# The opening of a decoder block: the exponential behind the root, one quarter of the squares on VectorE, the root ahead of the weight's split, the first value products by high parts first

## The chip, the cores and the metric

The kernel runs on one core of a Trainium2 chip. That core has TensorE (matrix products, PE in the profile), VectorE (DVE), ScalarE (ACT), GpSimd (POOL), SyncE (SP, which issues most loads) and 16 DMA engines. The metric is the device time of one execution in microseconds; less is better. A time before or after is the median of several executions.

## The reference

One layer of a hybrid decoder block on 2048 tokens of width 1024, all in float32. A conditioning vector gives a shift, a scale and a gate; the normed input is projected to eight pieces; one branch is a gated linear recurrence (RG-LRU), the other attention over three dilated windows; both are merged and added to the input.

```python
mod = c_act @ w_mod[l] + b_mod[l]                       # c_act = silu(c)
shift, scale, gate = jnp.split(mod, 3, axis=-1)
h = rms_norm(x, g_norm[l]) * (1.0 + scale[:, None, :]) + shift[:, None, :]
proj = h @ w_in[l]
x_rnn, z_rnn, q, k, v, z_attn, g_r, g_a = jnp.split(proj, IN_SPLITS, axis=-1)
...                                                     # conv, RG-LRU, attention, merge
x = x + gate[:, None, :] * (merged @ w_o[l])
return rms_norm(x, g_final)
```

`rms_norm` divides each row by the root of its mean square. In the RG-LRU, `log_a = -8 * r * softplus(-lam)`; `softplus(-lam)` is a constant of 1024 channels.

## The kernel before

Each large product is done in three matmuls: a number is split in a high part that TensorE takes exactly and a low part, and high by high, high by low and low by high are summed (`mm3`). For a weight, ScalarE copies the high part (`hi_act`, L162) and GpSimd subtracts it from the whole for the low part (`lo_pool`, L168); for the activations VectorE subtracts (`lo_dve`, L171). `S` are the tiles of split weights.

All products use a Strassen-like scheme on blocks of the sequence and the width. The order of the work isn't left to a scheduler: it is the order in which the program is written, engine by engine. An engine works through its own list, and waits at an instruction until what that needs is there. SyncE issues the loads in the written order.

The opening, lines 614 to 865, brings the first 512 rows of x (`x0`, four row sets of 128 rows by 1024) to a normed and shifted form, and makes the first products, of the values v, with them. Its parts are:

- `decay_constants` (L681) makes the constant `softplus(-lam)` on 128 x 8 elements. It is a generator, and is continued by `next(decay)`. ScalarE makes the exponential (L690), VectorE a series in 25 small operations (L694 to L705). Before each function of another family ScalarE loads a table (`ACT_TABLE_LOAD`).
- The squares of x0 (L711 to L713) are summed by row on ScalarE. `rstd_first` (L173) forms the mean on VectorE and the square root on ScalarE (L176). `rstd_last` (L178) inverts it and refines it with one Newton step on 128 x 4 elements (L180 to L184). `scale_rows` (L782) multiplies the rows of x, the first 256 columns of all four row sets first, the other 768 later.
- `mod_rows`, `mod_products` and `mod_turned` compute `c_act @ w_mod`, 256 columns of shift and scale at a time (index j from 0 to 3). Of eight blocks of 128 rows of the weight, ScalarE and VectorE sum the first 3, 4, 6 or 8 (by j) scaled by `ca` into `acc` (L730, L734), TensorE takes the others. The sum leaves as a row, `mrow` (ScalarE, L745), is turned to a column by eight one-column matmuls, and VectorE adds the bias (`mod`, L755) and the gain (`gs`, L756).
- `even(j)` transposes two blocks of 128 columns of x0 on TensorE (`turned`, L542). For each, ScalarE applies scale and shift twice, once to the high part (L552) and once to the full number (L556), and VectorE subtracts for the low part (L171).
- `value_sums(j, units)` (L766) adds to six sums in PSUM, called X, X, Z, W, V, Y, the products of those two blocks, 12 matmuls of 128 x 256 for each sum; the two X come first.
- `splits(m, j)` splits a weight tile of v, and loads the next. `idle_matmuls(n)` runs n matmuls of no use on a constant tile.

The PSUM pool `pg` has two buffers. Every tile that is asked from it, of `idle_matmuls`, `mod_products`, `mod_turned` and `turned` alike, waits until the tile before the last has been read.

Of the kernel before, what the change touches and what calls it, by code (L numbers as in the profile page):

```python
# [15 lines left out]
ALU = mybir.AluOpType  # L16
# [73 lines left out]
def decoder_block(ctx, tc, x, c, positions, g_norm, w_mod, b_mod, w_in, b_gate, conv_w, conv_b,  # L90
# [62 lines left out]
    def mm(o, l, r, st, sp, **kw):  # L153
        nc.tensor.matmul(o, lhsT=l, rhs=r, start=st, stop=sp, **kw)  # L154
# [18 lines left out]
    def rstd_first(ss):  # L173

        nc.vector.tensor_scalar(ss[:, 0], ss[:, 0], 1.0 / D, EPS, ALU.mult, ALU.add)
        nc.scalar.activation(ss[:, 1], ss[:, 0], AF.Sqrt)  # L176
# [451 lines left out]
    def load_mod(j):  # L628
        for q in range(2):
            w_m[q, j] = t = T(hp, [P, KT, 256], F32, "T", bufs=14)  # L630
            c0 = q * D + j * 256
            nc.sync.dma_start(t[:], w_mod[0, :, c0 : c0 + 256].rearrange("(k p) m -> p k m", p=P))
# [35 lines left out]
    def splits(m, j):  # L668
        split_raw(m, j)
        if ahead:  # L670
            load_raw(*ahead.pop(0))
# [11 lines left out]
    def decay_constants():  # L683
        nc.vector.tensor_scalar(hb[:], par[:, C_BG : C_BG + 16], 0.5, None, ALU.mult)
        la = par[:, C_LAM : C_LAM + 8]
        e1 = T(cp, [P, 8], F32, "e1")
        e2 = T(cp, [P, 8], F32, "e2")
        e3 = T(cp, [P, 8], F32, "e3")
        nc.vector.scalar_tensor_tensor(e1[:], la, -1.0, la, ALU.mult, ALU.min)
        nc.scalar.activation(e1[:], e1[:], AF.Exp)  # L690
        yield
        nc.vector.tensor_scalar(e2[:], e1[:], 2.0, None, ALU.add)
        nc.vector.reciprocal(e2[:], e2[:])
        nc.vector.tensor_tensor(e1[:], e1[:], e2[:], ALU.mult)  # L694
        nc.vector.tensor_tensor(e2[:], e1[:], e1[:], ALU.mult)
        nc.vector.tensor_scalar(e3[:], e2[:], 1.0 / 19, 1.0 / 17, ALU.mult, ALU.add)
        for d in (15, 13, 11, 9, 7, 5, 3, 1):
            if d == 9:
                yield
            nc.vector.tensor_tensor(e3[:], e3[:], e2[:], ALU.mult)  # L700
            nc.vector.tensor_scalar(e3[:], e3[:], 1.0 / d, None, ALU.add)
        nc.vector.tensor_tensor(e3[:], e3[:], e1[:], ALU.mult)
        nc.vector.tensor_scalar(e1[:], la, -1.0, 0.0, ALU.mult, ALU.max)
        nc.vector.scalar_tensor_tensor(e1[:], e3[:], 2.0, e1[:], ALU.mult, ALU.add)
        nc.vector.tensor_scalar(sp8[:], e1[:], 8.0, None, ALU.mult)  # L705
# [2 lines left out]
    next(decay)  # L708
    ssx = T(vx, [P, 3, 4], F32, "ssx", bufs=2)
    nc.scalar.activation(ssx[:, 1, 0:1], ones[:], AF.Sqrt)  # L710
    for r in range(4):  # L711
        jk = T(vx, [P, D], BF16, "hf", bufs=2)
        nc.scalar.activation(jk[:], x0[r], AF.Square, accum_out=ssx[:, 0, r : r + 1])  # L713
    load_mod(2)
    splits(0, 0)
    load_mod(3)

    mod = T(cp, [P, 2, KT], F32, "mod")
    sh = mod[:, 0, :]
# [39 lines left out]
    def even(j):  # L759
        for k in (2 * j, 2 * j + 1):  # L760
            build(vx, ("B11", "B21"), x0, k, True, pt=turned(x0, k))
# [4 lines left out]
    def value_sums(j, units):  # L766

        for m, g in units:
            for r in range(2):
                js = slice((2 * g + r) * P, (2 * g + r + 1) * P)  # L770
                for k in (2 * j, 2 * j + 1):
                    (hh, hl), w = B[("B11", "B21")[k // KH]], w_v[m, j]
                    mm3(sums[m, g][:, r, :], hh[:, k % KH, js], hl[:, k % KH, js], w[:, 0, k % 2], w[:, 1, k % 2],
                        first=j == 0 and r == 0 and k == 0, last=j == 3 and k == KT - 1, skip_group_check=True)

    def squares(xs):
        ss = T(vx, [P, 3, 4], F32, "ssx", bufs=2)
        for r in range(4):
            jk = T(vx, [P, D], BF16, "hf", bufs=2)
            nc.scalar.activation(jk[:], xs[r], AF.Square, accum_out=ss[:, 0, r : r + 1])  # L780
        return ss

    def scale_rows(xs, ss, rows=range(4), cols=slice(0, D)):
        for r in rows:
            nc.vector.tensor_scalar(xs[r][:, cols], xs[r][:, cols], ss[:, 1, r : r + 1], None, ALU.mult)
# [10 lines left out]
    def first_values():  # L796

        odd = build_odd(vx, x1)
        units = list(sums)
        for q in range(2):  # L800
            mod_rows(0, q)
        next(decay)
        mod_products(0)
        idle_matmuls(3)
        rstd_first(ssx)
        splits(1, 0)
        x1.extend(load_x(hp, 1, "T", 14))
        rstd_last(ssx)
        scale_rows(x0, ssx, cols=slice(0, 2 * P))
        mod_turned(0)  # L810
        even(0)
        for q in range(2):
            mod_rows(1, q)
        splits(2, 0)
        scale_rows(x0, ssx, cols=slice(2 * P, D))
        mod_rows(2, 0)
        next(decay, None)
        for j in range(4):
            for i, (m, g) in enumerate(units):
                value_sums(j, [(m, g)])  # L820
                if j < 3 and g:
                    splits(m, j + 1)
                if j == 3:
                    if i:
                        store_values(vx, *old, sums[old[0], old[2]])
                    old = m, 0, g
                    if i < 4:
                        split_raw(3, i)
                    if i in (3, 5):
                        next(odd)  # L830
                if (j, i) == (2, 1):
                    ss = squares(x1)
                    rstd_first(ss)
                if i == 2 and j < 3:
                    mod_products(j + 1)
                    if j == 2:
                        rstd_last(ss)
                        scale_rows(x1, ss, range(2))
                if i == 3 and j < 3:
                    mod_turned(j + 1)  # L840
                    even(j + 1)
                    if j == 0:
                        mod_rows(2, 1)
                        mod_rows(3, 0)
                        mod_rows(3, 1, 0, 4)
                    elif j == 1:
                        mod_rows(3, 1, 4)
                    else:
                        scale_rows(x1, ss, range(2, 4))
        spare[0] = True  # L850
        plan = {(t, i): [] for t in range(5) for i in range(4)}
        for i in range(4):
            plan[0, i].append(lambda i=i: load_piece(0, i))
            for t in range(1, 4):
                plan[t, i].append(lambda t=t, i=i: split_piece(t - 1, i))
                if t < 3:
                    plan[t, i].append(lambda t=t, i=i: load_piece(t, i))
            plan[4, i].append(lambda i=i: products(i - 4))
        for t, i in ((0, 0), (0, 2), (1, 0), (1, 1), (1, 3), (2, 0), (2, 1), (2, 3), (3, 0), (3, 1)):
            plan[t, i].append(lambda: next(odd))  # L860
        plan[3, 2].append(lambda: (next(odd, None), products(-8)))
        plan[3, 3].append(lambda: products(-5))
        evicts = [lambda: store_values(vx, *old, sums[old[0], old[2]])]
        value_runs(vx, ((3, 0), (3, 1), (0, 1), (1, 1), (2, 1)), plan, evicts)
        products(0)
# [1478 lines left out]
```

## Time and profile before

| | us |
|---|---|
| median of 3 executions | 2202.35 (2197.92, 2202.59, 2202.35) |
| the profiled execution | 2203.34 |
| its span, first to last instruction | 2200.7 |
| TensorE busy in the span | 2161.4 (98%) |
| VectorE, ScalarE, GpSimd busy | 1488.3, 1261.9, 1237.5 |
| first high part of x0 starts (ScalarE, L552) | 23.57 |
| second mod read (VectorE, L755) | 40.31 |

In the rows of a timeline the first number is the start in microseconds from the start of the span and the second the duration of all instructions of the row (xN at its end is their count). Then come the engine, the line, the operation, and what it writes and reads. A bracket gives the idle time of the engine just before, and what ended it.

### The profile page before, as it was taken

How to read it: one execution, taken by the hardware profiler on the slowest of the kernel's cores; microseconds unless marked ns; L12 is line 12 of the kernel's file. 1: busy time of each engine (PE TensorE's matmuls, PEld its weight loads, DVE VectorE, ACT ScalarE, POOL GpSimd, SP SyncE). 2: the span in 40 equal slices, each digit the busy share in tenths (PEclk: the TensorE clock that was granted, in tenths of full speed). 3: DMA queues.
4: the chain of work that ended last, by engine and by line, in shares of the span. 5: the costliest groups of instructions: out<-in, count | busy, mean ns of one | idle time of the engine just before them, and what ended most of it. 6: DMA issues, size and time to landing. Idle time of an engine off the chain costs nothing. (4 is left out here: it accounts for less than half of the span.)

```text
span 2200.7 us, 34270 instructions
## 1 busy us (share of the span) xinstructions
PE 2161.4 (98%) x11330; PEld 1838.1 (84%) x11330; DVE 1488.3 (68%) x2453; ACT 1261.9 (57%) x2543; POOL 1237.5 (56%) x910
## 2 busy tenths in 40 slices
PE   8999999999999999999999999999999999999998
PEld 5998888888888998888888887888889898978786
DVE  6678888978576765455545465467677878755876
ACT  4647667667543447557557412567778887632433
POOL 2468767677566355445445223446575656433886
PEclk9999999999999999999999999999999999999999
DMA  8355665665897567787887898989988888799453
GB/s 291 103 172 185 219 198 194 203 209 195 265 274 221 166 191 255 248 250 233 263 258 248 263 286 274 284 267 273 289 272 270 242 257 255 226 291 296 160 164 134
DMA packets 454522, 513.89 MB, mean 234 GB/s; under 512 B 91241, under 2 KB 333637, under 8 KB 453577
## 3 DMA queue, kind: packets, MB, share of 16 engines
q1 hardware_dynamic: 427444, 431.81, 65.2%
q10 hardware_dynamic: 26708, 79.86, 9.4%
q8 instruction: 89, 1.46, 0.3%
q14 instruction: 89, 0.72, 0.1%
q0 software_dynamic: 192, 0.05, 0.0%
HBM read 337.52 MB, written 174.07 MB: 232 GB/s over the span
## 5 line engine op out<-in xcount | busy, mean ns | idle before, releaser
L168 POOL TENSOR_TENSOR S<-R,S 128x512 fp32r<-128x512 f32 x278 | 411.4, 1485 | 372.2 <-ACT S L162 271.2
L154 PE MATMUL V<-T,S 128*128 128x512 f32 x1344 | 324.4, 390 | 0.5 <-DVE xr L482 0.5
L154 PE MATMUL X<-T,S 128*128 128x512 f32 x1344 | 323.3, 389 | 0.3 <-POOL S L168 0.3
L154 PEld LDWEIGHTS X<-T,S 128*128 128x128 f32 x1344 | 252.0, 188 | 52.9 <-POOL S L168 0.7
L154 PEld LDWEIGHTS V<-T,S 128*128 128x128 f32 x1344 | 251.4, 188 | 52.9 <-DVE xr L482 1.0
L154 PE MATMUL pj<-yh,S 128*128 128x512 f32 x848 | 287.6, 397 | 4.4 <-ACT yh L162 3.8
L168 POOL TENSOR_TENSOR S<-s,S 128x512 fp32r<-128x512 f32 x114 | 183.0, 1605 | 103.2 <-ACT S L162 78.7
L162 ACT ACTIVATE S<-R 128x512 fp32r<-128x512 f32 x278 | 171.2, 622 | 117.1 <-DMA R<-in_w_in_dram 77.4
L154 PEld LDWEIGHTS pj<-yh,S 128*128 128x128 f32 x848 | 160.7, 190 | 37.5 <-ACT yh L162 4.7
L1596 ACT ACTIVATE pp<-pp,st 128x256 f32<-128x256 f32 (+3 forms) x256 | 133.4, 523 | 75.4 <-DVE st L1595 75.0
L154 PE MATMUL pj<-yl,S 128*128 128x512 f32 x424 | 167.5, 395 | 2.4 <-DVE yl L171 1.5
L154 PE MATMUL Y<-T,S 128*128 128x512 f32 x672 | 161.5, 389 | 0.0
L154 PE MATMUL W<-T,S 128*128 128x512 f32 x672 | 161.5, 389 | 0.0
L154 PE MATMUL Z<-T,S 128*128 128x512 f32 x672 | 161.4, 389 | 0.0
L154 PEld LDWEIGHTS Z<-T,S 128*128 128x128 f32 x672 | 126.1, 188 | 26.2
L154 PEld LDWEIGHTS Y<-T,S 128*128 128x128 f32 x672 | 126.1, 188 | 26.2
L154 PEld LDWEIGHTS W<-T,S 128*128 128x128 f32 x672 | 126.1, 188 | 26.2
L162 ACT ACTIVATE S<-s 128x512 fp32r<-128x512 f32 x114 | 71.1, 624 | 117.2 <-DVE s L299 61.6
L998 DVE SCALAR_TENSOR_TENSOR xc<-xr,par,xc 128x512 f32<-128x512 f32 x96 | 97.9, 1020 | 50.6 <-ACT xc L992 48.3
L171 DVE TENSOR_TENSOR ptl<-pT,pth 128x384 fp32r<-128x384 f32 (+1 forms) x160 | 97.8, 627 | 49.3 <-ACT pth L162 47.1
L1595 DVE CUSTOM_DVE_ANT_0 pp<-sc,msk 128x256 f32<-128x256 f32 (+3 forms) x256 | 104.2, 449 | 34.7 <-PE sc L154 32.1
L168 POOL TENSOR_TENSOR kq<-kraw,kq 128x512 fp32r<-128x512 f32 (+1 forms) x64 | 101.3, 1594 | 39.8 <-ACT kq L162 30.2
(393 smaller groups left out, 4828.7 us busy)
## 6 DMA issues: line engine op xcount, KB each, us to landing
sD<-S ACTq DMA_DIRECT2D x112, 512.0 KB, 3.6
S<-sD SPq DMA_DIRECT2D x112, 512.0 KB, 4.8
S<-wD SPq DMA_DIRECT2D x100, 512.0 KB, 5.9
R<-in_w_in_dram SPq DMA_DIRECT2D x195, 256.0 KB, 4.2
wD<-s ACTq DMA_DIRECT2D x64, 256.0 KB, 4.5
T<-in_w_mod_dram SPq DMA_DIRECT2D x8, 1024.0 KB, 9.5
vN<-ev SPq DMA_DIRECT2D x64, 128.0 KB, 2.6
zaT<-ev SPq DMA_DIRECT2D x32, 256.0 KB, 3.4
```

Source lines behind the costliest of these rows:

```text
L154: nc.tensor.matmul(o, lhsT=l, rhs=r, start=st, stop=sp, **kw)
L162: nc.scalar.activation(o, i, AF.Copy)
L168: nc.gpsimd.tensor_tensor(o, i, h.bitcast(F32), ALU.subtract)
L171: nc.vector.tensor_tensor(o, i, h.bitcast(F32), ALU.subtract)
L998: nc.vector.scalar_tensor_tensor(xc, xr[:, i : i + CH], cw(i), xc, ALU.mult, ALU.add)
L1595: nc.vector.tensor_tensor_reduce(pdst, s_ps, mask, 1.0, 3e38, ALU.add, ALU.min, m_)
L1596: nc.scalar.activation(pdst, pdst, AF.Exp, bias=m_, scale=-1.0, accum_out=l_)
```

## The change

It rearranges the opening and nothing else.

1. The exponential of the decay constants, which stood ahead of the squares, comes behind the split of weight (2, 0). A dummy square root behind it brings the root's table back, so ScalarE loads four tables in the opening where it loaded three. VectorE's series comes in two pieces behind the second and the third reading of mod; it stood in two pieces ahead of the first and the second.
2. Of the four row sets' squares, the third is made on VectorE, with one multiply-and-sum.
3. The root of x0 stands directly behind the last square. The row copy `mrow` of the first mod follows, and the split of weight (0, 0), which stood ahead of both, comes after it.
4. Three idle matmuls are added between the turning of the first mod and the first transposes.
5. The first two X sums are made in the order: all products of high activations, of the first block and then of the second, then the products of low activations.

On ScalarE, behind the sigmoid of the conditioning vector and its table, the rows were (ssx holds mean squares and roots, hf the squares, S_39 and S_58 the splits of weights (0, 0) and (1, 0)):

```order
L690 ACT_TABLE_LOAD
L690 ACTIVATE e_29_176<-e_29_176 128x8
L710 ACT_TABLE_LOAD
L710 ACTIVATE ssx_181<-ones_64 128x1
L713 ACTIVATE hf_183,ssx_181<-T_100 128x1024
L713 ACTIVATE hf_185,ssx_181<-T_100 128x1024
L713 ACTIVATE hf_187,ssx_181<-T_103 128x1024
L713 ACTIVATE hf_189,ssx_181<-T_103 128x1024
L162 ACTIVATE S_39_195<-R_17_148 128x512
L745 ACTIVATE mrow_248<-pg_235 1x512
L176 ACTIVATE ssx_181<-ssx_181 128x4
L162 ACTIVATE S_58_256<-R_18_150 128x512
```

The same place of ScalarE's list now (S_54 is the split of weight (0, 0)):

```order
L712 ACT_TABLE_LOAD
L712 ACTIVATE ssx_180<-ones_64 128x1
L719 ACTIVATE hf_182,ssx_180<-T_100 128x1024
L719 ACTIVATE hf_184,ssx_180<-T_100 128x1024
L719 ACTIVATE hf_212,ssx_180<-T_103 128x1024
L176 ACTIVATE ssx_180<-ssx_180 128x4
L751 ACTIVATE mrow_229<-pg_216 1x512
L162 ACTIVATE S_54_235<-R_17_148 128x512
L162 ACTIVATE S_58_244<-R_18_150 128x512
```

One table load, the exponential and one square are gone from ahead of the root (L176), and the split and the row copy stand behind it.

On TensorE, from the first transposes of x0 (L542) into the first X sum, the rows were, with what each waits for (T_144 holds high and T_145 low activations):

```order
L542 MATMUL pg_281<-cs_62,T_100 128x128 [waits DMAHW5_49,DVE_49]
L542 MATMUL pg_281<-cs_62,T_100 128x128 [waits DMAHW7_49,DVE_49]
L542 MATMUL pg_281<-cs_62,T_103 128x128 [waits DMAHW0_49,DVE_49]
L542 MATMUL pg_281<-cs_62,T_103 128x128 [waits DMAHW1_49,DVE_49]
L542 MATMUL pg_290<-cs_62,T_100 128x128 [waits DVE_49]
...
L154 MATMUL X_206<-S_39_195,T_144 128x256 [waits Activation_49]
L154 MATMUL X_206<-S_39_195,T_144 128x256 [waits Pool_49]
L154 MATMUL X_206<-S_39_195,T_145 128x256 [waits DVE_49]
L154 MATMUL X_206<-S_39_195,T_144 128x256 [waits Activation_49]
```

And now, in the same place:

```order
L542 MATMUL pg_273<-cs_62,T_100 128x128 [waits DMAHW5_49,DVE_49]
L542 MATMUL pg_273<-cs_62,T_100 128x128 [waits DMAHW7_49]
L542 MATMUL pg_273<-cs_62,T_103 128x128 [waits DMAHW0_49]
...
L154 MATMUL X_192<-S_54_235,T_144 128x256 [waits Activation_49]
L154 MATMUL X_192<-S_54_235,T_144 128x256 [waits Pool_49]
L154 MATMUL X_192<-S_54_235,T_144 128x256 x2
L154 MATMUL X_193<-S_54_235,T_144 128x256 x4
L154 MATMUL X_192<-S_54_235,T_144 128x256 [waits Activation_49]
...
L154 MATMUL X_192<-S_54_235,T_145 128x256 [waits DVE_49]
```

The four transposes no longer wait for VectorE one by one: the first has a single wait that stands for its buffer of `pg`, and so for the reading of the mod that lay there, behind all four scalings on VectorE. The first product with a low activation, which was third, now stands behind 16 with high ones.

On VectorE, between the accumulations of the second mod and the low parts of the next two blocks, the rows were (e are the series' tiles):

```order
L704 SCALAR_TENSOR_TENSOR e_29_176<-e_31_178,e_29_176 128x8
L705 TENSOR_SCALAR sp_28_174<-e_29_176 128x8
L755 TENSOR_TENSOR mod_204<-pg_410,par_63 128x2x2
L756 SCALAR_TENSOR_TENSOR gs_205<-mod_204,par_63 128x2
L171 TENSOR_TENSOR T_145<-hf_423,T_144 128x512
```

And now, with seven of the series' operations left out:

```order
L761 TENSOR_TENSOR mod_190<-pg_390,par_63 128x2x2
L762 SCALAR_TENSOR_TENSOR gs_191<-mod_190,par_63 128x2
L694 TENSOR_SCALAR e_30_177<-e_29_176 128x8
L695 RECIPROCAL e_30_177<-e_30_177 128x8
...
L702 TENSOR_TENSOR e_31_178<-e_31_178,e_30_177 128x8
L703 TENSOR_SCALAR e_31_178<-e_31_178 128x8
L171 TENSOR_TENSOR T_145<-hf_414,T_144 128x512
```

Fourteen operations are gone from ahead of this reading of mod, and eleven stand behind it, ahead of the low parts; the other fourteen stand in the same way behind the next reading. GpSimd's and SyncE's lists are as before.

```diff
         nc.vector.scalar_tensor_tensor(e1[:], la, -1.0, la, ALU.mult, ALU.min)
+        yield
         nc.scalar.activation(e1[:], e1[:], AF.Exp)
+        nc.scalar.activation(e2[:, 0:1], ones[:], AF.Sqrt)
         yield
...
-    for r in range(4):
+
+    def square(r):
         jk = T(vx, [P, D], BF16, "hf", bufs=2)
-        nc.scalar.activation(jk[:], x0[r], AF.Square, accum_out=ssx[:, 0, r : r + 1])
+        if r == 2:
+            nc.vector.tensor_tensor_reduce(jk[:], x0[r], x0[r], 1.0, 0.0, ALU.mult, ALU.add, ssx[:, 0, r : r + 1])
+        else:
+            nc.scalar.activation(jk[:], x0[r], AF.Square, accum_out=ssx[:, 0, r : r + 1])
+    square(0)
+    square(1)
     load_mod(2)
-    splits(0, 0)
-    load_mod(3)
...
+    def first_sums(units):
+
+        def matmuls(k, hl, parts):
+            for m, g in units:
+                for r in range(2):
+                    js = slice((2 * g + r) * P, (2 * g + r + 1) * P)
+                    for i in parts:
+                        mm(sums[m, g][:, r, :], B["B11"][hl][:, k, js], w_v[m, 0][:, i, k],
+                           r == k == hl == i == 0, False, skip_group_check=True)
+        for hl, parts in ((0, (0, 1)), (1, (0,))):
+            for k in range(2):
+                matmuls(k, hl, parts)
...
         for q in range(2):
             mod_rows(0, q)
-        next(decay)
+        square(2)
+        square(3)
+        rstd_first(ssx)
         mod_products(0)
         idle_matmuls(3)
-        rstd_first(ssx)
+        splits(0, 0)
+        load_mod(3)
         splits(1, 0)
         x1.extend(load_x(hp, 1, "T", 14))
         rstd_last(ssx)
         scale_rows(x0, ssx, cols=slice(0, 2 * P))
         mod_turned(0)
+        idle_matmuls(3)
         even(0)
         for q in range(2):
             mod_rows(1, q)
         splits(2, 0)
         scale_rows(x0, ssx, cols=slice(2 * P, D))
+        next(decay)
         mod_rows(2, 0)
-        next(decay, None)
         for j in range(4):
             for i, (m, g) in enumerate(units):
-                value_sums(j, [(m, g)])
+                if j or m:
+                    value_sums(j, [(m, g)])
+                elif not g:
+                    first_sums(units[:2])
...
                 if i == 3 and j < 3:
                     mod_turned(j + 1)
+                    if j < 2:
+                        next(decay, None)
                     even(j + 1)
```

## The prediction

> **What bounds the kernel now.** The page's first part and the stretches by clock window come first.
>
> ```profile
> PE 2161.4 (98%) x11330; PEld 1838.1 (84%) x11330; DVE 1488.3 (68%) x2453; ACT 1261.9 (57%) x2543; POOL 1237.5 (56%) x910
> ```
>
> ```profile
> 18.45:21.86 3.41, 1.05 (x8) 0.96 (x8) 2.32 (x7) 1.47 (x4) 2.48 (x2) 1.00 1.09 349
> 21.86:25.27 3.41, 2.91 (x10) 1.97 (x10) 1.59 (x7) 1.70 (x3) 0.00 (x0) 0.50 1.09 348
> ...
> 28.69:32.10 3.41, 3.41 (x18) 3.41 (x18) 3.34 (x5) 0.80 (x2) 1.83 (x2) 0.50 1.09 348
> 32.10:35.51 3.41, 3.41 (x21) 1.89 (x21) 3.30 (x8) 0.00 (x0) 0.00 (x0) 1.00 1.09 347
> ```
>
> In the second view the columns behind the length are PE, PEld, DVE, ACT and POOL busy, then the granted clock. TensorE works 98% of the span, so a microsecond saved elsewhere counts only where TensorE stands idle or slow, and that is the opening. In 18.45 to 21.86 it issued eight one-column matmuls, and the clock then stayed at 0.50 from 21.86 to 32.10. The change touches only this opening; on every engine the rest keeps its order. So the question is how much earlier the opening ends.
>
> Who holds TensorE there is read from the timelines, VectorE (DVE) first:
>
> ```profile
> 18.35 0.17 DVE L175 TENSOR_SCALAR ssx<-ssx 128x4 f32<-128x4 f32 x1 [2.07 <-ACT hf L713]
> 19.44 0.18 DVE L180 RECIPROCAL ssx<-ssx 128x4 f32<-128x4 f32 x1 [0.92 <-ACT ssx L176]
> 19.65 0.55 DVE L181 TENSOR_TENSOR ssx<-ssx 128x4 f32<-128x4 f32 x1
> 20.23 1.19 DVE L182 TENSOR_TENSOR ssx<-ssx 128x4 f32<-128x4 f32 x1
> ...
> 21.86 1.14 DVE L785 TENSOR_SCALAR T<-T,ssx 128x256 f32<-128x256 f32 x4
> 22.91 0.15 DVE L755 TENSOR_TENSOR mod<-pg,par 128x4 f32<-128x4 f32 x1
> ```
>
> ```profile
> 11.14 1.28 ACT L690 ACT_TABLE_LOAD   x1
> ...
> 12.66 1.28 ACT L710 ACT_TABLE_LOAD   x1
> ...
> 17.18 1.04 ACT L713 ACTIVATE hf<-T 128x1024 bf16<-128x1024 f32 x1
> ...
> 18.22 0.61 ACT L162 ACTIVATE S<-R 128x512 fp32r<-128x512 f32 x1
> ...
> 19.22 0.19 ACT L176 ACTIVATE ssx<-ssx 128x4 f32<-128x4 f32 x1
> ...
> 23.57 0.78 ACT L552 ACTIVATE T<-pg,mod,gs 128x512 fp32r<-128x512 f32 x1 [3.64 <-PE pg L542]
> ...
> 37.78 0.59 ACT L745 ACTIVATE mrow<-pg 1x512 f32<-1x512 f32 x1 [8.29 <-PE pg L154]
> ```
>
> ```profile
> 18.92 2.48 POOL L168 TENSOR_TENSOR S<-R,S 128x512 fp32r<-128x512 f32 x2 [14.32 <-ACT S L162]
> 27.74 1.40 POOL L168 TENSOR_TENSOR S<-R,S 128x512 fp32r<-128x512 f32 x1 [6.34 <-ACT S L162]
> 29.56 1.39 POOL L168 TENSOR_TENSOR S<-R,S 128x512 fp32r<-128x512 f32 x1 [0.42 <-ACT S L162]
> ```
>
> The chain is: four squares on ScalarE (ACT), v on VectorE, the root, its refinement, the scaling of x's first columns, transposes, the first high part at 23.57. Two detours lie in it. The root stands behind a split and a row copy on ScalarE (recip idles 0.92). And L181 and L182, on four columns, take 0.55 and 1.19 while GpSimd (POOL) subtracts from 18.92 to 21.40; the second ends 0.02 behind POOL.
>
> **The change, part by part.** For the root alone, the same work on the next 512 rows, and the load of the fourth row set:
>
> ```profile
> 62.93 0.17 DVE L175 TENSOR_SCALAR ssx<-ssx 128x4 f32<-128x4 f32 x1 [0.57 <-ACT hf L780]
> 63.38 0.18 DVE L180 RECIPROCAL ssx<-ssx 128x4 f32<-128x4 f32 x1 [0.27 <-ACT ssx L176]
> ...
> 64.39 2.42 DVE L785 TENSOR_SCALAR T<-T,ssx 128x1024 f32<-128x1024 f32 x2
> ```
>
> ```profile
> L530 SPq DMA_DIRECT2D T<-in_x_dram x1: 327/327/327, 7.7 to 7.7; - x1
> DMA to landing us min/median/max: 7.9/7.9/7.9
> ```
>
> ```profile
> L998 DVE SCALAR_TENSOR_TENSOR xc<-xr,par,xc 128x512 f32<-128x512 f32 x96 | 97.9, 1020 | 50.6 <-ACT xc L992 48.3
> ...
> L1595 DVE CUSTOM_DVE_ANT_0 pp<-sc,msk 128x512 f32<-128x512 f32 x32 | 22.0, 687 | 2.1
> ```
>
> *Squares.* Without the first table load and the exponential ScalarE's squares may begin 12.66 − 11.14 = 1.52 earlier, and there are three. The last still waits for the fourth row set, which lands at 7.7 + 7.9 = 15.6, so it starts there and not at 17.18: 1.55 gained. VectorE's square has no row in this trace. The fused operation L1595 (687 ns per 512) would make it 1.4 us for 1024, the two-input L998 (1020) 2.0. Begun when its tile is there, near 14.4, it ends by 15.8 or 16.4, before the last square (16.65): cost nothing at either bound. I take 1.4, since L1595 is a fused operation with a reduction, as this one is. That cover gone, each microsecond would come off the 1.55.
>
> *Root.* v to recip takes 63.38 − 62.93 = 0.45 with ScalarE free, against 19.44 − 18.35 = 1.09: 0.64 gained. Recip stands at 17.25, 2.19 earlier.
>
> *Refinement.* Recip to scaling takes 64.39 − 63.38 = 1.01 with POOL idle, against 21.86 − 19.44 = 2.42. POOL's first subtraction now comes behind root, row copy and split, near 18.2, so the four columns escape it: 1.41 gained. The scaling may begin at 18.26, 3.60 earlier.
>
> *Scaling.* It now runs into the same two POOL operations, 18.2 to 20.7. None held: mod is read at 18.26 + 1.05 = 19.3, a gain of 3.6. All held: 20.7 + 1.05 = 21.75, a gain of 1.15. L181 shows that one VectorE operation passes between two of POOL's, and the first scaling starts about with POOL, so I take one left behind POOL: 20.7 + 0.28, mod at 21.0, 1.9 gained. The Trainium skill (SBUF — State Buffer, "Who interferes with whom") says that VectorE and GpSimd share a port pair as an exclusive lock, that a tensor_scalar in a 2-port mode contends for it and that whoever issues first keeps it for the whole instruction. By that rule the scaling would keep 1.15 to 1.9; without it 3.6. L182, ending with POOL, agrees for two-input operations.
>
> *Transposes.* They no longer follow each scaled row: three idle matmuls take a PSUM buffer, so the first transposes wait until mod is read. The idle matmuls themselves lie in TensorE's wait. Two hundred nanoseconds of the 1.9 go here; the first high part comes at 21.85 instead of 23.57, 1.7 gained.
>
> Then the sums, TensorE and VectorE:
>
> ```profile
> 24.40 0.80 PE L154 MATMUL X<-S,T 128*128 128x256 f32 x2
> 25.79 1.01 PE L154 MATMUL X<-S,T 128*128 128x256 f32 x3 [0.60 <-DVE T L171]
> 27.13 4.42 PE L154 MATMUL X<-S,T 128*128 128x256 f32 x19 [0.33 <-DVE T L171]
> 31.35 1.92 PE L154 MATMUL Z<-S,T 128*128 128x256 f32 x12
> 33.20 3.61 PE L154 MATMUL pg<-T,ca 128*1 128x256 f32 x16
> ...
> 39.23 1.05 PE L154 MATMUL pg<-ones,mrow 1*128 1x1 f32 x8
> ...
> 44.01 3.04 PE L154 MATMUL X<-S,T 128*128 128x256 f32 x24
> ```
>
> ```profile
> 26.39 0.69 DVE L171 TENSOR_TENSOR T<-hf,T 128x512 fp32r<-128x512 f32 x1 [0.65 <-ACT hf L556]
> 27.00 4.76 DVE L734 SCALAR_TENSOR_TENSOR acc<-T,ca,acc 128x256 f32<-128x256 f32 x6
> 31.67 2.20 DVE L785 TENSOR_SCALAR T<-T,ssx 128x768 f32<-128x768 f32 x4
> 33.79 2.56 DVE L734 SCALAR_TENSOR_TENSOR acc<-T,ca,acc 128x256 f32<-128x256 f32 x5
> 36.26 0.16 DVE L700 TENSOR_TENSOR e<-e,e 128x8 f32<-128x8 f32 x1
> ...
> 38.90 0.17 DVE L705 TENSOR_SCALAR sp<-e 128x8 f32<-128x8 f32 x1
> 40.31 0.16 DVE L755 TENSOR_TENSOR mod<-pg,par 128x4 f32<-128x4 f32 x1 [1.24 <-PE pg L154]
> ...
> 42.38 0.69 DVE L171 TENSOR_TENSOR T<-hf,T 128x512 fp32r<-128x512 f32 x1 [1.71 <-ACT hf L556]
> 43.72 0.69 DVE L171 TENSOR_TENSOR T<-hf,T 128x512 fp32r<-128x512 f32 x1 [0.64 <-ACT hf L556]
> ```
>
> *High parts first.* The second low part ends at 27.08, and 19 of the 24 X matmuls stood behind it. Counted from the high part (27.08 − 23.57 = 3.51) it now ends at 25.4, with four matmuls behind it: at 3.04/24 = 0.127 each X ends at 25.9 instead of 31.35. If the clock is still 0.5, some 0.22 each (4.42/19) for 16 high matmuls and the four give 28.0. Z takes 1.5 warm. From 33.20 the row products, sums and W run 7.1 to the next mod (40.31), which therefore comes at 25.9 + 1.5 + 7.1 = 34.5 warm, 37 or a little over cold.
>
> *VectorE to the same mod.* From 27.00 to 36.26 are 9.26 us of products and scaling; the 14 small operations behind (to 39.07, 2.8 us) leave. From 25.3 that gives 34.6, with POOL's two holds as before: six products in 4.76 against five in 2.56 are 1.7 too long. Without holds it is 32.9; another half-held scaling gives 35.5. TensorE and VectorE are thus late together near 34.5, and a POOL operation then falls into the scaling of the remaining columns. I take mod at 35.3: 5.0 earlier.
>
> *Small operations and tables.* The first eleven (0.205 apart, 2.25 us) go behind this mod, into the idle 1.71 + 0.64 = 2.35 ahead of its low parts: free. The other 14 (2.8) go behind the next mod, into a gap of the same make: 0.4 over. Exponential, two table loads and a dummy root (3.0 together) come behind the split of (2,0), in the 8.29 us that ScalarE idles before 37.78; the accumulator and split behind them come 3 us later, still ahead of the first products that read them. That cover gone, 3.0 would be lost. The Trainium skill (ScalarE: Activation LUTs, "What ACT_TABLE_LOAD costs") counts 2.66 us for a switch with its drain and so speaks against the extra switch; two switches by that would be 5.3, still within 8.29. Here the next instruction followed its 1.28 at once.
>
> Sum: −5.0 + 0.4 = −4.6. The profiled execution takes 2203.34 (span 2200.7), so 2198.7; the median of the three runs, 2202.35, lies 1.0 below, so 2197.8. What a measurement can tell from no change is about 0.2%, 4.4 us; the forecast lies just past that.
>
> **Rivals.**
> - *Clock and locks both kind.* The idle matmuls and the earlier high matmuls fill the window, the clock opens one window sooner, and the scaling passes POOL. Half the difference between 3.6 and 1.9 (0.85), one of POOL's two holds on the products gone (0.85), and TensorE's path warm and 0.85 earlier put the second mod near 33.6: gain 6.7 less 0.4, so 2196. For it: only eight one-column matmuls filled the window. Against: VectorE's own 9.26 us.
> - *Locks and clock both unkind.* All scalings held (0.75 later), X cold, and mod at 37 or 37.8: gain 2.5 to 3.3 less 0.4, 2199.5. For it: 28.69 to 32.10 was wholly busy and yet at 0.50.
> - *The root doesn't move:* VectorE's square or the fourth row's landing takes 1.5 more than reckoned. Root order and high parts alone remain, less than 2: near 2201.
> - *Slower, by the clock.* The new wait for mod leaves TensorE idle in other windows. A closed window of 3.41 costs half, 1.7; the idle stretch above closed three, 5.1. Two such more, 10.2, against 4.6 won: 2208. It decides from the sixth additional closed window. For it: a window with 2.91 us of work didn't reopen the clock. Against: this work is denser than before.
>
> **Numbers.** Forecast (gain 4.0 to 5.6) 0.44, of it 0.31 past 4.4; kind 0.22; unkind 0.22; root unmoved 0.04; slower 0.08. Faster by over 0.2%: 0.31 + 0.22 = 0.53; within: 0.13 + 0.22 + 0.04 = 0.39; slower 0.08. The range leaves out the slower case and the far ends: 2193.5 (both bounds: 3.6 and 32.9, gain 8.8) to 2202.8.
>
> **What would show it.** Right: recip near 17.2, L181 and L182 at 0.16 each, mod near 21.0, the first high part near 21.9, X done by 28, the second mod near 35.3, ScalarE idle before its row copy still above zero. Wrong: recip above 18.5; the scaling held past 21.75; X running beyond 29 at half clock; a second mod above 38; or clock windows at 0.5 where there were none.

## The result and the profile after

| | before | changed |
|---|---|---|
| median of 8 executions | 2200.71 (2197.92 to 2202.59) | 2195.18 (2193.28 to 2200.47) |
| profiled execution, span | 2203.34, 2200.7 | 2195.18, 2193.4 |
| TensorE busy | 2161.4 | 2156.6 |

The ratio is 0.998, with a 95% interval of 0.9971 to 0.9988: 2.6 to 6.4 us won. The time lies inside the range that was given, 2.6 below the forecast. In the later runs below, in which the kernel before was run along, its median was 2199.1 to 2199.4; the changed kernel was not run again there.

In both profiles the opening ends with the third round of V, behind the reading of the fourth mod; from there TensorE works on nearly without a break. It starts 3.77 earlier. Before and changed:

```profile
67.35 1.68 PE L154 MATMUL V<-S,T 128*128 128x256 f32 x12
```

```profile
63.58 1.68 PE L154 MATMUL V<-S,T 128*128 128x256 f32 x12
```

Nearly all of the other 3.5 us by which the two spans differ comes from one place late in the program, as GpSimd's and TensorE's timelines show. The GpSimd rows (POOL) are the same work in both kernels, and so are the rows W. Before:

```profile
1776.52 1.59 POOL L168 TENSOR_TENSOR wh<-vraw,wh 128x640 fp32r<-128x640 f32 x1 [5.40 <-PE sc L154]
```

```profile
2049.87 2.56 PE L154 MATMUL X<-F,S 128*128 128x512 f32 x10 [0.63 <-POOL S L168]
2055.17 2.50 PE L154 MATMUL V<-F,S 128*128 128x512 f32 x7 [2.73 <-DVE xo L2207]
2058.59 2.50 PE L154 MATMUL V<-F,S 128*128 128x512 f32 x5 [0.93 <-POOL F L168]
2060.90 3.90 PE L154 MATMUL Z<-F,S 128*128 128x512 f32 x12
2064.64 2.88 PE L154 MATMUL W<-F,S 128*128 128x512 f32 x12
```

Changed:

```profile
1772.51 1.57 POOL L168 TENSOR_TENSOR wh<-vraw,wh 128x640 fp32r<-128x640 f32 x1 [5.40 <-PE sc L154]
```

```profile
2049.85 4.86 PE L154 MATMUL V<-F,S 128*128 128x512 f32 x12 [2.69 <-DVE xo L2235]
...
2057.26 2.88 PE L154 MATMUL W<-F,S 128*128 128x512 f32 x12
```

At 1776 the lead is 4.0; at W it is 7.4. In between the kernel before waited twice more for GpSimd, 0.63 and 0.93, and had its clock at 0.50 for two stretches, the changed one for one. That code is the same in both. In the other profiles the number of such stretches behind the opening was 2 to 6, whatever the edit; so only the 3.8 belongs to the change by the profile, and the medians agree with that within their interval. Each kernel has one profiled execution.

The opening of the changed kernel, VectorE and GpSimd first:

```profile
17.45 0.18 DVE L180 RECIPROCAL ssx<-ssx 128x4 f32<-128x4 f32 x1 [0.27 <-ACT ssx L176]
17.67 0.16 DVE L181 TENSOR_TENSOR ssx<-ssx 128x4 f32<-128x4 f32 x1
17.86 0.16 DVE L182 TENSOR_TENSOR ssx<-ssx 128x4 f32<-128x4 f32 x1
...
18.46 3.25 DVE L804 TENSOR_SCALAR T<-T,ssx 128x256 f32<-128x256 f32 x4
21.63 0.15 DVE L761 TENSOR_TENSOR mod<-pg,par 128x4 f32<-128x4 f32 x1
...
26.21 3.87 DVE L740 SCALAR_TENSOR_TENSOR acc<-T,ca,acc 128x256 f32<-128x256 f32 x6
30.00 3.21 DVE L804 TENSOR_SCALAR T<-T,ssx 128x768 f32<-128x768 f32 x4
33.13 3.62 DVE L740 SCALAR_TENSOR_TENSOR acc<-T,ca,acc 128x256 f32<-128x256 f32 x5
36.67 0.15 DVE L761 TENSOR_TENSOR mod<-pg,par 128x4 f32<-128x4 f32 x1
```

```profile
18.50 2.53 POOL L168 TENSOR_TENSOR S<-R,S 128x512 fp32r<-128x512 f32 x2 [13.93 <-ACT S L162]
26.96 1.40 POOL L168 TENSOR_TENSOR S<-R,S 128x512 fp32r<-128x512 f32 x1 [5.93 <-ACT S L162]
31.15 1.64 POOL L168 TENSOR_TENSOR S<-R,S 128x512 fp32r<-128x512 f32 x1 [2.79 <-ACT S L162]
34.69 1.26 POOL L168 TENSOR_TENSOR S<-R,S 128x512 fp32r<-128x512 f32 x1 [1.90 <-ACT S L162]
```

The root's chain is as forecast, with recip at 17.45 and the two products at 0.16. Then the four scalings, 1.14 before, take 3.25 beside GpSimd's 2.53. On ScalarE the last square waits for the fourth row set, and the first high part starts 0.79 earlier than before:

```profile
15.83 1.06 ACT L719 ACTIVATE hf<-T 128x1024 bf16<-128x1024 f32 x1 [1.03 <-DMA T<-in_x_dram]
...
22.78 0.78 ACT L552 ACTIVATE T<-pg,mod,gs 128x512 fp32r<-128x512 f32 x1 [3.85 <-PE pg L542]
```

TensorE's side, and below it the stretches by clock window, with the columns as in the prediction:

```profile
21.83 1.77 PE L542 MATMUL pg<-cs,T 128*128 128x128 f32 x8 [2.08 <-DVE mod L761]
23.61 3.95 PE L154 MATMUL X<-S,T 128*128 128x256 f32 x24
27.40 1.60 PE L154 MATMUL Z<-S,T 128*128 128x256 f32 x12
...
34.96 1.05 PE L154 MATMUL pg<-ones,mrow 1*128 1x1 f32 x8
```

```profile
18.67:22.08 3.41, 1.33 (x8) 0.70 (x9) 3.27 (x6) 0.27 (x1) 2.36 (x2) 1.00 1.09 348
22.08:25.50 3.42, 3.40 (x17) 3.00 (x16) 0.69 (x1) 2.72 (x5) 0.00 (x0) 0.50 1.10 349
25.50:28.91 3.41, 3.41 (x29) 3.30 (x28) 3.23 (x5) 3.38 (x7) 1.40 (x1) 1.00 1.09 347
```

X runs without a wait, and the clock is at 0.50 for one stretch instead of three. Z starts 3.95 earlier than before.

### The profile page after: what moved, and what is told of

Same layout as the page of the kernel before. It is cut to its first block, busy times and chain, and to the rows that moved or that the text cites. A ratio compares the mean times of both kernels' runs of the same rounds, so it can differ in the third digit from the quotient of the medians.

```text
span 2193.4 us, 34275 instructions
## 1 busy us (share of the span) xinstructions
PE 2156.6 (98%) x11332; PEld 1833.7 (84%) x11333; DVE 1491.1 (68%) x2455; ACT 1261.4 (58%) x2543; POOL 1239.5 (57%) x910
## 4 chain that ended last, share of the span: by engine, by line
PE 60%; DMA 7%; DVE 4%; POOL 3%; issue 3%; SPq 1%; ACT 1%; POOLq 0%; ACTq 0%; DVEq 0%
PE X L154 12%; PE V L154 11%; PE pj L154 9%; PE W L154 7%; PE Z L154 7%; PE Y L154 6%; PE sc L154 3%; PE o L154 3%; PE pg L154 1%; DMA R<-oT 1%; DMA S<-wD 1%; PE pT L1708 1%; POOL kq L168 1%; DMA meT<-fg 1%; DMA fg<-mrT 1%
```

## The experiments

One row for each kernel's one profile. "Halved" counts the clock stretches of 3.41 at 0.50 in the opening. The second mod is read when two lists are through: TensorE's (the end of the one-column matmuls) and VectorE's (the end of what stands ahead of the reading, which is the reading's start less the idle time that the row shows). The third round of V shows what is left of it.

| kernel | halved | Z starts | TensorE's list | VectorE's list | second mod | third V | median |
|---|---|---|---|---|---|---|---|
| before | 3 | 31.35 | 40.28 | 39.07 | 40.31 | 67.35 | 2200.71 |
| changed | 1 | 27.40 | 36.01 | 36.67 | 36.67 | 63.58 | 2195.18 |
| sums_by_thirds | 3 | 30.89 | 39.88 | 36.01 | 39.91 | 66.95 | 2197.54 |
| high_first_alone | 2, and 1 at 40.9 | 28.67 | 37.28 | 40.15 | 40.15 | 68.01 | 2199.18 |
| series_ahead | 2 | 28.16 | 36.77 | 38.95 | 38.95 | 66.16 | 2197.66 |
| split_before_root | 1 | 26.68 | 35.29 | 35.53 | 35.53 | 62.41 | 2192.90 |
| squares_on_act | 2 | 28.75 | 37.35 | 35.95 | 37.39 | 64.43 | 2195.94 |
| exp_first | 2 | 29.16 | 37.76 | 36.18 | 37.79 | 64.83 | 2195.88 |
| no_idle | 2 | 27.72 | 36.32 | 35.41 | 36.36 | 63.40 | 2195.78 |
| scale_on_act | 1 | 25.89 | 34.50 | 34.89 | 34.89 | 61.89 | 2193.32 |
| sbr_idle7 | 0 | 26.49 | 35.10 | 36.03 | 36.03 | 62.92 | 2194.34 |
| sbr_idle7_rows | 0 | 26.27 | 34.88 | 35.03 | 35.03 | 62.06 | 2193.40 |
| act_scale_rows | 0 | 25.45 | 34.06 | 34.81 | 34.81 | 61.88 | 2192.09 |
| act_scale_rows2 | 0 | 25.22 | 33.82 | 34.76 | 34.76 | 61.77 | 2194.37 |

The theory to test was: two lists end close together ahead of the second mod, and the change had to shorten both. Its rivals were that one part carries the gain, or the clock alone.

**The sums in the old order.**

```diff
-                if j or m:
-                    value_sums(j, [(m, g)])
-                elif not g:
-                    first_sums(units[:2])
+                value_sums(j, [(m, g)])
```

> One part undone: the first two X sums in the old order, three parts of a product after another, the rest as changed. In the changed kernel the second low part ends at 26.29, X at 27.40, and the second mod is read at 36.67 by a VectorE that does not idle, 0.7 behind the last of the one-column matmuls that make it (35.94). Theory A (VectorE's list sets the second mod): X ends later, at about 26.3 + 19 x 0.127 = 28.7 with the clock open, the row products 1.3 later, and since 0.7 of that is slack the second mod is read 0.6 later; the fourth mod at 63.3 to 63.6 instead of 62.97, the time +0.3 to +0.8. Theory B (X's tail sets it, as the reordering is meant to cure): the clock is again half for 19 matmuls, X ends at 30 or later, second mod 2.5 or more later, the time +2.5 to +4.

B: X again took 4.42 for its last 19 matmuls, the clock was at 0.50 for three stretches, and VectorE waited for TensorE:

```profile
26.67 4.42 PE L154 MATMUL X<-S,T 128*128 128x256 f32 x19 [0.33 <-DVE T L171]
```

```profile
39.91 0.16 DVE L761 TENSOR_TENSOR mod<-pg,par 128x4 f32<-128x4 f32 x1 [3.90 <-PE pg L154]
```

The third V starts at 66.95, 0.40 ahead of the kernel before; the time, 0.9992 (0.9983 to 1.0) of it, can't be told from it. Without this part nearly all of the opening's gain is gone. Theory A had the clock open too early.

**The high parts first, alone.** The kernel before with `first_sums`, and nothing else.

```diff
                 if j or m:
                     value_sums(j, [(m, g)])
+                elif not g:
+                    first_sums(units[:2])
```

> One part alone: the kernel before with only the first two X sums by high parts first. Undone alone, this part cost the changed kernel 3.4 of its 3.8 (fourth mod at 66.34 against 62.97, and 66.73 before). Theory A (parts need each other): the stretch from 21.86 still holds the transposes' wait and stays short of the 3.3 busy that opened the clock so far, the next one is now full, so the clock opens one window sooner (28.7 instead of 32.1); X ends near 29.5 instead of 31.35; the second mod can't come before VectorE's list reaches it at 39.1 (40.31 less the 1.24 that it idled), so the fourth mod comes 1.0 to 1.3 earlier, 65.5 to 65.8, and the time falls by 1.2. Theory B (this part carries it by itself): fourth mod 3.0 to 3.6 earlier, the time -3.4.

The third V came 0.66 later than before, the time was 1.0003 (0.9993 to 1.0013). Z starts 2.7 earlier and TensorE's list ends 3.0 earlier. It then stands, since the series still lies ahead of VectorE's reading:

```profile
37.21 0.66 PE L542 MATMUL pg<-cs,T 128*128 128x128 f32 x4
40.36 0.66 PE L542 MATMUL pg<-cs,T 128*128 128x128 f32 x4 [2.48 <-DVE mod L755]
40.77 2.81 PE L154 MATMUL V<-S,T 128*128 128x256 f32 x12
```

```profile
37.47:40.89 3.42, 0.94 (x9) 0.70 (x8) 2.55 (x17) 0.30 (x1) 0.00 (x0) 1.00 1.08 414
40.89:44.30 3.41, 3.41 (x19) 3.41 (x18) 1.58 (x3) 3.41 (x7) 0.00 (x0) 0.50 0.99 389
```

The stretch of that wait held 0.94 of matmuls, and the next had the clock at 0.50; V took 2.81 instead of 1.68. A wait has taken the place of the one removed, and cost more than the 0.16 won at the mod. Theory A was right that the parts need each other, and short of the clock's price.

**The series one place earlier.**

```diff
         next(decay)
         mod_rows(2, 0)
+        next(decay)
         for j in range(4):
```

> The changed kernel with the series one place earlier on VectorE: its eleven operations (2.25) ahead of the second mod's reading, its fourteen (2.8) behind it, none behind the third. Theory A (VectorE's list sets the second mod, and room made there is what lets the earlier X sums count): the second mod 2.0 to 2.3 later than the changed kernel's 36.67, TensorE idle ahead of the transposes by about 2 with perhaps a halved stretch behind, as where the high parts alone came first; the fourth mod 2 to 4 later, the time +2 to +4. Theory B (TensorE's own work sets it and VectorE has slack): second mod up to 0.5 later, the time +0.5 at most.

A: the second mod 2.28 later, TensorE idle 1.81 ahead of it, the third V 2.58 later, the time 2.5 above the changed kernel's median and 0.9996 (0.9987 to 1.0005) of the kernel before. TensorE's wait of 1.81 halved no stretch, unlike the 2.48 above. The three runs together: TensorE's list was shortened by the order of the sums, VectorE's by the series' new place, and each without the other leaves 0.4 to 1.2 of 3.8, or less than nothing.

**The split ahead of the root.**

```diff
         square(3)
-        rstd_first(ssx)
-        mod_products(0)
-        idle_matmuls(3)
         splits(0, 0)
         load_mod(3)
+        mod_products(0)
+        idle_matmuls(3)
+        rstd_first(ssx)
```

> One part undone: the split of weight (0, 0) and the loads behind it stand ahead of the root again, the rest as changed. Theory A (GpSimd holds whatever VectorE does then, and has only moved its hold from the refinement to the scaling): GpSimd starts about 0.7 earlier (17.7), the two products of the refinement are held (0.5 to 1.2 instead of 0.16), the scaling starts near 20.3 and runs free in 1.1; the first mod is read at 21.3 to 21.9, where the changed kernel has 21.63; the time within 0.5 of the changed kernel. Theory B (the root's place carries the gain): the first mod 1.5 to 2.2 later and the second with it, the time +1.5 to +2.

A, and more: by the profile this order is better than the changed kernel's. The third V starts 1.17 earlier, the time is 2192.90, 0.9968 (0.9956 to 0.998) of the kernel before; that interval and the changed kernel's overlap.

```profile
18.01 0.55 DVE L181 TENSOR_TENSOR ssx<-ssx 128x4 f32<-128x4 f32 x1
18.59 1.19 DVE L182 TENSOR_TENSOR ssx<-ssx 128x4 f32<-128x4 f32 x1
...
20.22 1.14 DVE L804 TENSOR_SCALAR T<-T,ssx 128x256 f32<-128x256 f32 x4
21.27 0.16 DVE L761 TENSOR_TENSOR mod<-pg,par 128x4 f32<-128x4 f32 x1
```

GpSimd holds the small products as it did before the change, and is through when the scaling starts; the first mod is read 0.36 earlier than in the changed kernel. But x0's last row set landed earlier in this execution, and the last square started 0.31 earlier, at 15.52. Counted from there the first mod comes after 5.75 here and 5.80 there: the hold has only moved. The transposes also run beside the scaling again (from 20.67, ahead of the mod), and the first high part starts at 21.78 instead of 22.78. Counted from the last square again, the high part comes 0.69 earlier and the third V 0.86. The three idle matmuls are still there, so they alone don't make the transposes wait for the mod; what does isn't shown.

**All squares on ScalarE.**

```diff
-        if r == 2:
+        if r < 0:
             nc.vector.tensor_tensor_reduce(jk[:], x0[r], x0[r], 1.0, 0.0, ALU.mult, ALU.add, ssx[:, 0, r : r + 1])
```

> One part undone: all four squares on ScalarE, the rest as changed. Theory A (the landing of the fourth row set at 15.8 ends the wait): ScalarE makes the third square in the 1.03 it idled before the last (14.7 to 15.8), the last still starts at 15.8, recip at 17.45; time +0 (within 0.3). Theory B (VectorE's square saves a square's time): recip 1.0 later, first mod up to 1.0 later, the time up to +1.0.

A as to the root: recip at 17.53 against 17.45, the last square at 15.90, when the fourth row set is there. The third V came 0.85 later all the same: here the transposes start 0.5 behind the start of the clock's stretch (21.37), which therefore holds only 2.86 of work, and a second stretch is halved. That this comes of the edit isn't shown, since the stretches start at another place in each execution. The time, 2195.94, can't be told from the changed kernel's.

**The exponential ahead of the squares.**

```diff
+        nc.scalar.activation(e1[:], e1[:], AF.Exp)
         yield
-        nc.scalar.activation(e1[:], e1[:], AF.Exp)
-        nc.scalar.activation(e2[:, 0:1], ones[:], AF.Sqrt)
-        yield
...
         scale_rows(x0, ssx, cols=slice(2 * P, D))
-        next(decay)
         mod_rows(2, 0)
```

> One part undone: the exponential with its table stands ahead of the squares again, VectorE still makes the third square and its series stays where the change put it. Theory A: the three squares start at 14.15 instead of 12.63 and the last at 16.2 instead of 15.83 (0.4 later, since the landing had already held it to 15.83); root, split and GpSimd's hold all 0.4 later, the second mod 0.4 later, the time +0.4. ScalarE's idle time before its second row copy grows from 2.4 to about 5, which nobody feels. Theory B (1.5 of the change come from here): the last square at 17.2, the time +1.5.

A: the last square at 16.23, recip 0.40 later. Here too two stretches were halved, and the third V came 1.25 later; the time, 2195.88, can't be told from the changed kernel's. The last square starts at 17.18 before, at 16.23 with VectorE's square alone, at 15.90 with the exponential moved alone and at 15.83 with both: either alone brings most of it.

In these two runs TensorE's list ends last, 1.4 and 1.6 behind VectorE's, since X took 5.02 and 5.12 with two halved stretches; in the changed kernel, with one, it ended 0.7 ahead. Where the stretches fall differs between executions, so by these profiles the opening's gain is 2.5 to 3.8, and not one fixed number.

**Without the idle matmuls.**

```diff
         mod_turned(0)
-        idle_matmuls(3)
         even(0)
```

> The changed kernel without the three idle matmuls ahead of the first transposes. Theory A (they fill 0.8 of a stretch that halves the clock anyway, and VectorE sets the second mod): the stretch before 22 holds some 0.5 instead of 1.33, the clock is halved for one or two stretches as in the runs so far, the transposes may follow each scaled row again; the fourth mod within 0.8 of 62.97, the time within 0.8 of the changed kernel. Theory B (they carry the clock): the clock halved for three stretches as before the change, X's end near 30, fourth mod 2.5 or more later, the time +2.5 or more.

A: two stretches halved, X ends about 0.3 later, but the transposes don't wait for the mod and the third V starts 0.18 earlier. The time can't be told from the changed kernel's. Whether the idle matmuls spare a stretch isn't shown, since the stretches start elsewhere here (at 19.77).

**The first scaling on ScalarE.**

```diff
+    def scale_act(xs, ss, rows=range(4), cols=slice(0, D)):
+        for r in rows:
+            nc.scalar.activation(xs[r][:, cols], xs[r][:, cols], AF.Copy, scale=ss[:, 1, r : r + 1])
...
-        scale_rows(x0, ssx, cols=slice(0, 2 * P))
+        scale_act(x0, ssx, cols=slice(0, 2 * P))
```

> The changed kernel with the first 256 columns scaled on ScalarE, which idles there, in place of VectorE. Theory A (GpSimd's hold on VectorE's scaling, 3.25 for four operations that take 1.14 elsewhere, is what keeps the first high part at 22.78): ScalarE scales from 18.95 in some 0.4 each and is through by 20.6, mod is read near 18.6, the first high part starts at 20.8 to 21.2, 1.6 to 2.0 earlier; the second mod and the fourth follow by 1.2 to 2.0 (fourth near 61.3 instead of 62.97), the time 2193 to 2194 where the changed kernel has 2195.2. Theory B (no hold; the scaling waits for something else, as x's landing or the row's turning): first high part within 0.5 of 22.78, the time the same.

A:

```profile
19.05 1.69 ACT L809 ACTIVATE T<-T,ssx 128x256 f32<-128x256 f32 x4
21.30 0.78 ACT L552 ACTIVATE T<-pg,mod,gs 128x512 fp32r<-128x512 f32 x1 [0.57 <-PE pg L542]
```

ScalarE took 1.69 beside the same GpSimd work beside which VectorE took 3.25. The first high part starts 1.48 earlier, the third V 1.69 earlier; the time is 2193.32, 0.9974 (0.9964 to 0.9984) of the kernel before.

**Seven idle matmuls.** In the kernel with the split ahead of the root.

```diff
         mod_turned(0)
-        idle_matmuls(3)
+        idle_matmuls(7)
```

> The run with the split ahead of the root again, with seven idle matmuls instead of three ahead of the first transposes. There the stretch 18.32 to 21.73 was 2.26 busy, and the clock stood at 0.50 in the next one (21.73 to 25.15). Theory A (idleness in one stretch halves the clock of the next): four more of 0.27 each bring it to 3.3, the clock is never halved in the opening, the first X sums take 3.0 to 3.3 instead of 4.24, the first high part comes 0.2 earlier; the second mod, for which VectorE does not idle, gains 0.2 to 0.5; the time -0.2 to -0.8 against that run. Theory B (the clock is halved by something else than idleness, say by the one-row matmuls): the clock in 21.7 to 25.2 stays 0.50 and nothing moves.

A as to the clock: it was never halved in the opening, here and in the next run, which has the seven too, and X took 3.51 instead of 4.24. (Two runs further down show the same with three, so the number of idle matmuls isn't what decides alone.) But nothing came of it. x0's last row set landed 0.5 later in this execution; counted from the first high part, the second mod comes after 13.71 here and 13.75 there, since VectorE's list ends last in both. The time, 2194.34, lies 1.4 above that run's, where up to 0.8 less was expected.

**A quarter of the accumulation earlier.**

```diff
         mod_turned(0)
+        mod_rows(1, 0)
         idle_matmuls(7)
         even(0)
-        for q in range(2):
-            mod_rows(1, q)
+        mod_rows(1, 1)
```

> As the run with seven idle matmuls, and the first quarter of the second mod's accumulation (one copy on ScalarE, three operations on VectorE) written ahead of the first high parts, into the 1.6 that VectorE idles there. Theory A (VectorE's list sets the second mod): VectorE reaches it 1.5 earlier, TensorE's row then ends last, and the mod gains 0.8 to 1.4 against the run without it; fourth mod near 60.3. Theory B (TensorE's list sets it already): under 0.3 gained.

A: from the first high part to the second mod 12.92 instead of 13.71, 0.8 gained at the mod; the third V 0.86 earlier (0.2 of it from an earlier landing), at 62.06, short of the hope of 60.3 for the mod ahead of it (61.45). The time is 0.9977 (0.9967 to 0.9988) of the kernel before.

**Both together.** The scaling on ScalarE, and the quarter early, its first operation on VectorE.

```diff
-    def mod_rows(j, q, a=0, b=KT):
+    def mod_rows(j, q, a=0, b=KT, dve=False):
...
-            if j:
+            if j and not dve:
...
         mod_turned(0)
+        mod_rows(1, 0, dve=True)
         idle_matmuls(3)
         even(0)
-        for q in range(2):
-            mod_rows(1, q)
+        mod_rows(1, 1)
```

> The run with the first scaling on ScalarE, and the first quarter of the second mod's accumulation (four operations, 1.9) on VectorE ahead of the first low parts, where it then idles from 19.6 to 22.8. If VectorE's list sets the second mod there (0.4 of TensorE's waiting was for it), it comes 0.4 to 1.2 earlier and the fourth near 60.3 to 60.9 instead of 61.28, the time near 2192.5. If TensorE's list sets it: within 0.3 of that run.

The second mod came only 0.08 earlier and the third V 0.01. TensorE's list isn't the reason, as it ends at 34.06. VectorE has a new wait, and GpSimd's hold behind it:

```profile
27.47 2.20 DVE L804 TENSOR_SCALAR T<-T,ssx 128x768 f32<-128x768 f32 x4
30.32 4.57 DVE L740 SCALAR_TENSOR_TENSOR acc<-T,ca,acc 128x256 f32<-128x256 f32 x5 [0.65 <-ACT acc L736]
34.81 0.15 DVE L761 TENSOR_TENSOR mod<-pg,par 128x4 f32<-128x4 f32 x1
```

Its five operations for the third mod must wait for ScalarE's copy, and then take 4.57 beside two GpSimd operations (4.34 in the run with the scaling alone, 2.56 where they ran free). What the copy waits for, ScalarE's row shows:

```profile
29.79 0.51 ACT L736 ACTIVATE acc<-T,ca 128x256 f32<-128x256 f32 x1 [1.38 <-DMA T<-in_w_mod_dram]
```

It waits for the third mod's weight to land. The median is 2192.09, 0.9972 (0.996 to 0.9983) of the kernel before: the lowest of all, below both kernels, though not to be told from the run with the scaling alone or the one with the split ahead of the root.

**Half of the second scaling on ScalarE too.**

```diff
-        scale_rows(x0, ssx, cols=slice(2 * P, D))
+        scale_rows(x0, ssx, range(2), cols=slice(2 * P, D))
+        scale_act(x0, ssx, range(2, 4), cols=slice(2 * P, D))
```

> As the run before, with two of the four row sets' remaining columns scaled on ScalarE as well, ahead of its table loads (two operations of about 0.9): VectorE's list loses 1.1 to 1.6. If it still set the second mod by more than that: 0.5 to 1 earlier. If TensorE's list sets it by now, as I expect: within 0.3 of the run before, or up to 0.8 later where ScalarE's loads delay the third mod's accumulation.

The second mod came at 34.76 against 34.81: the scaling left on VectorE is 1.05 shorter, and its wait for the copy grew from 0.65 to 1.85. Not TensorE's list, as I expected, but this wait sets the mod now. Here the copy doesn't idle for the landing:

```profile
29.63 0.20 ACT L692 ACTIVATE e<-ones 128x1 f32<-128x1 f32 x1
29.74 0.49 ACT L736 ACTIVATE acc<-T,ca 128x256 f32<-128x256 f32 x1
```

It follows at once on ScalarE's own list, which the two scalings have made 1.75 longer, and which ends within 0.2 of the weight's landing (near 29.6). So two causes end together here: the load, and ScalarE's work ahead of the copy. The median, 2194.37, is 0.9977 (0.9966 to 0.9987) of the kernel before, and can't be told from that run's.

## Why the prediction was right, and where it was not

- **Sign, size and range** held: 2195.18 against 2197.8, 5.5 won where 4.6 were forecast. That the medians' gain lies between 4.0 and 5.6, as forecast, is in part luck. The opening gave 3.8 by the profile, so the sum was 0.8 too large for it. The forecast started from a median of three, 2202.35, where eight gave 2200.71; against the later medians of 2199.1 to 2199.4 the same 2195.18 is 3.9 to 4.2 less. In the pair of profiles the waits and the clock late in the program, which was reckoned only as a loss, hide the 0.8.
- **Squares** (1.55 reckoned): the last started at 15.83, 1.35 earlier, held by the landing. VectorE's square took 1.23, near the 1.4 that was taken from the fused row. That it costs nothing was right; that it also brings nothing beyond what the exponential's move brings, the run with all squares on ScalarE shows.
- **Root and refinement** (2.19 and 1.41): recip came 1.99 earlier, and the two products escaped GpSimd.
- **Scaling** (1.9 of possible 1.15 to 3.6 taken): mis-sized; 1.28 was left. I had one scaling behind GpSimd's work, and there were two, since the one that began just ahead of it (18.46, GpSimd 18.50) was held too. By the lock that the Trainium skill describes (SBUF — State Buffer, "Who interferes with whom") the gain is 1.15 to 1.9, which holds here. That whoever issues first keeps the port for the whole instruction doesn't show in the first scaling: by the profile it began 0.04 ahead of GpSimd and took 1.45, where a free one takes 0.34.
- **Transposes** (0.2 reckoned for the new wait): mis-sized. From the mod to the first high part 1.15 pass, 0.66 before, half a microsecond. So the first high part came 0.79 earlier, not 1.7: 0.6 of what is missing is the scaling's, 0.3 the transposes'. These two terms of the sum failed together; with the split ahead of the root 0.7 of it is to be had.
- **High parts first**: X ended between my bounds of 25.9 and 28.0, near 27.4, with one halved stretch. That it carries nearly all of TensorE's share, and nothing alone, I had not said, though the two lists that end together stood in the working.
- **VectorE to the second mod** (35.3): 36.67, which is 3.64 earlier than before and not 5.0. Of the 1.4 that is missing 0.9 is the later first high part. Behind the low part its three groups take 10.46, not the 9.26 of before plus 0.7: GpSimd held one operation less among the six products (3.87 for 4.76), but one more in the scaling (3.21 for 2.20) and one more in the five (3.62 for 2.56).
- **Small operations and tables**: eleven free, as reckoned (the second low part 3.27 behind the mod, 3.41 before). The fourteen made the next X 0.26 longer, for which 0.4 stood; by the fourth mod (62.97, 3.76 earlier) that was gone. ScalarE still idled 2.43 before its row copy. The extra switch of tables cost nothing. The Trainium skill (ScalarE: Activation LUTs, "What ACT_TABLE_LOAD costs") counts a drain beside it; here the two switches took 26.90 to 29.90 with their functions, 3.0 as summed from rows, and no drain shows between them.
- **Of the rivals**, the unkind one came nearest: the second mod lies between its 37 and the forecast's 35.3, and X ran in part at the halved clock. The kind one's 33.6 didn't come, and the root moved. The slower one's mechanism is real: in the run with the high parts alone a new wait for the mod halved the clock and cost more than was won. In the changed kernel it found no wait longer than 0.29 at the second mod.

## What to carry to other kernels

Where two engines' lists end within a microsecond or two of each other ahead of a common step, shortening one buys a wait; look for the second list, and cost both edits together. Work that is moved out of the reach of a neighbour's hold should be followed to what that neighbour holds next: here the hold went from 1.4 on two tiny products to 2.1 on the scaling, and of what was tried only a change of engine removed it. A new wait can cost more than its length where the clock halves behind it: the one of 2.48 did, the one of 1.81 did not.

## What the hardware showed beyond that

- VectorE's in-place scaling by a row's factor and its products are held by GpSimd's subtraction one at a time: one VectorE operation passes between two of GpSimd's (a scaling of 256 columns took 0.34 free and 1.35 to 1.45 held, a product 0.48 and 1.37 to 1.60). ScalarE isn't held: its four scalings took 0.49 each beside the same GpSimd work.
- In the opening a halved clock came back after a stretch that was at least 3.29 busy (3.29 with the split ahead of the root), and not after 3.08 or less. Late in the program 2.88 brought it back once (without the idle matmuls, 2054.11 to 2057.53), and 3.27 once did not (a quarter earlier, 1428.00 to 1431.42). So the busy time alone doesn't decide it.
- Nor does it decide what halves the clock. A stretch of 1.60 with transposes and V's products kept it open (the series one place earlier, 37.27 to 40.68), and so did 2.44 with products of 256 columns (before, 15.03 to 18.45); 2.69 with eight one-column matmuls and transposes among it did not (the scaling on ScalarE, 17.12 to 20.53).
- The halved stretches of the opening start at 19.8 to 22.1 of the span, at another place in each execution. With X in the new order the opening met none, one or two of them, and X took 3.50 to 3.52, 3.92 to 4.24, or 4.58 to 5.12 (high parts alone 4.32).
